# TensorE in emission order through two encoder layers, with the attention steps rearranged and a split final sum

## The chip, the cores and the metric

The kernel runs on one core of a Trainium2 chip. The metric is the device time of the slowest (here the only) core in microseconds, as the median of several runs. The profiled execution is one run of its own, with its own time.

## The reference

Two layers of an encoder work on 16 meta tokens and 256 sequence tokens (T = 272) with 1024 channels, in float32. Each layer takes four token mixers from one normalised input, gates and sums them, and adds a gated feed-forward part:

```
u = rms_norm(h, ln_mix[l])
(aq, ak, av, bq, bk, bv, cq, ck, cv, dq, dzf, dzb, di, dg, gz) = split_in(u @ w_in[l])
y_a = windowed_sink_attention(...)   # 4 heads, relative bias, a sink in the softmax
y_b = axial_rope_attention(...)      # q and k normalised per head, then rotated
y_c = differential_attention(...)    # two softmaxes per head, p0 - lam * p1
y_d = hgrn2_bidirectional(...)       # gated linear recurrence, both directions
gate = sigmoid(gz)                   # 4 x 1024 columns of w_in
merged = sum over n of gate[n] * (y_n @ w_branch[l, n])
h = h + merged @ w_out[l]
u = rms_norm(h, ln_ffn[l])
h = h + (silu(u @ w_ffn_gate[l]) * (u @ w_ffn_up[l])) @ w_ffn_down[l]
out = rms_norm(h, ln_final)[meta tokens dropped]
```

## The kernel before

Every float32 product is made of three matmuls: weights and activations are each split into a high part (rounded to the format that TensorE takes at full pace) and a rest, and high*high, high*rest and rest*high are summed in PSUM. `split_next` (L261 to L279) loads one 512 KB weight tile on the SP queue, casts it on ScalarE (L275) and subtracts on VectorE (L276); `weights` keeps one tile ahead of the one in use, in three buffers. `block` makes one output tile of 128 channels from 24 matmuls of 272 columns (L290 to L292). In the second layer the gate products, branch products and the last feed-forward product are turned round (`prod_t`, L318 to L320), with 512 output columns to a matmul.

A layer begins with 22 projection blocks in the order `ORDER`. Two generators hang on that loop and on the loop after it, and `advance(a, b)` lets each go on by one step when its credit has reached 1:

- `branch_d` is mixer D: a step for the diagonal blocks (`close`, L721 and L733), seven steps for segment lengths 1 to 64 (`close` or `apart`, L749), one for the halves (L801, L802), one for the meta tokens (L815, L824), one for the product with the values (`mix`, L436 and L442) and one for the norm.
- `softmax_stream` is mixers C, B and A, in units of 128 queries. `scores` (L513) makes 12 matmuls on 64 rows each, in two groups of 6, each group into two PSUM tiles. VectorE reduces them, ScalarE takes the exponentials, `normalise` divides, `turn` (L453 to L460) transposes the probabilities, and `mix` multiplies them with the values. `close_unit` ran the division and the turning of a unit one after the other, as two steps, after the next unit's first scores.

`values` (L409 to L427) turns the value rows by transposes (L416) and small products (L425), and `prep_b` (L544 to L577) prepares mixer B's norms (L401, L562, L392). Both were called right after the projection block whose output they read had been scaled on VectorE (L963 or L965).

After the projections comes `MIXING`: gate blocks `g`, and branch products `w` of a mixer that is done. In the second layer `mixing_t` does this, and after each half of the last branch product it transposes the four 128-column tiles of that half of the sum (L889) and splits them (L891, L892) for the output product.

PSUM has two pools of four tiles: `pmm` for the large products and `pat` for everything else.

The order on each engine is made by a planner: it takes the instructions in the order in which the program emits them, but lets a later one go first where, by its own account of times, an earlier one isn't ready. The program on the engine then runs in that order.

The last feed-forward product of the second layer adds, for each of its 22 weight tiles, to four PSUM tiles (2 halves of the tokens by 2 halves of the channels); after it each half of the tokens is added to the rest (L1087), squared (L1089), its norm taken (L1090 to L1092), scaled with the norm and the final weights in one operation (L1094) and sent out (L1095).

Of the kernel before, what the change touches and what calls it, by code (L numbers as in the profile page):

```python
# [15 lines left out]
P = 128  # L16
# [28 lines left out]
RATE_D, RATE_S = 1.0, 1.0  # L45
WAIT_C = (8, 8)
# [35 lines left out]
def trunk(ctx, tc, xT, w_in, w_branch, w_out, w_gate, w_up, w_down, rel_bias, params, consts, masks, onehot, ln_out, out):  # L82
    nc = tc.nc
    V, S, G, PE = nc.vector, nc.scalar, nc.gpsimd, nc.tensor

# [458 lines left out]
    def prep_b(l, pj):  # L544

        src = [pj["bq0"], pj["bq1"], pj["bk"]]
        sqs = []
        for j in range(3):
            t = midt()
            S.activation(out=t, in_=src[j], func=AF.Square)  # L550
            sqs.append(t)
# [92 lines left out]
    def softmax_stream(l, c0, pj, done):  # L644
# [6 lines left out]
        def close_unit(u):  # L651
            n, qt, gen, st = u
            next(gen, None)
            yield
# [23 lines left out]
        for n, qt in units:  # L678
# [6 lines left out]
            next(gen)  # L685
            yield
            if pend:
                yield from close_unit(pend)
            if n == 2:
                next(gen)  # L690
                yield
            pend = (n, qt, gen, st)
        yield from close_unit(pend)


# [155 lines left out]
    def mixing_t(acts, rcol, done, advance):  # L851
# [3 lines left out]
        for kind, b, half in MIXING_T:  # L855
            n = BRANCHES[b]
            if kind == "g":
                pss = [pmm(), pmm()]
                for x in range(4):
# [4 lines left out]
                    advance(RATE_D, RATE_S)  # L864
# [9 lines left out]
            advance(RATE_D, RATE_S)  # L874
# [10 lines left out]
            if b == 3:  # L885
                for m in range(4 * half, 4 * half + 4):
                    ps = pat()
                    for i in range(2):
                        PE.transpose(ps[:, P * i:P * (i + 1)], acc[:, DM * i + P * m:DM * i + P * (m + 1)], ident)  # L889
                    t = slot(F32R)  # L890
                    S.copy(t[:, 0, META:], ps[:, :SEQ])  # L891
                    V.tensor_tensor(out=t[:, 1, META:], in0=ps[:, :SEQ], in1=t[:, 0, META:], op=ALU.subtract)  # L892
                    merged.append(t)
        return merged

    for l in range(DEPTH):
# [32 lines left out]
        for idx, name in enumerate(ORDER):  # L929
            t0 = first_token(l, name)  # L930
            ps = lead[idx] if idx < 3 else block(acts, t0)
            if l == 0 and idx == 3:
                prep_small()
            if name[:2] == "dz":
                d, j = name[2], int(name[3])
                z = midt()
                V.tensor_tensor(out=z[:, t0:], in0=ps[:, t0:T], in1=rstd[:, t0:], op=ALU.mult)
                dd = 0 if d == "f" else 1
                kdst, fdst = dt["KK"][:, 2 * dd + j, :], dt["T1"][:, 2 * (1 - dd) + j, :]
                if t0:  # L940
                    G.memset(kdst[:, :t0], 0.0)
                    G.memset(fdst[:, :t0], 1.0)
                fdst, kdst = fdst[:, t0:], kdst[:, t0:]
                S.activation(out=fdst, in_=z[:, t0:], func=AF.Sigmoid)
                S.activation(out=kdst, in_=z[:, t0:], func=AF.Sigmoid, scale=-1.0)
                if l > 0:
                    c = 2 * dd + j
                    V.tensor_scalar(out=fdst, in0=fdst, scalar1=lbc[:, c:c + 1], scalar2=lb[:, c:c + 1], op0=ALU.mult, op1=ALU.add)
                    V.tensor_scalar(out=kdst, in0=kdst, scalar1=lbc[:, c:c + 1], scalar2=None, op0=ALU.mult)
                V.tensor_scalar(out=fdst, in0=fdst, scalar1=1e-30, scalar2=None, op0=ALU.max)  # L950
                continue
            if name[0] == "d":
                dst = dt[name[1]][:, int(name[2]), :]
            else:
                half = 1 if name[1] == "v" or name[-1] == "1" else 0
                if half == 0:
                    cur = pj[name[:2]] = slot()
                dst = pj[name] = cur[:, half, :]
            scale = {"aq": 0.125, "cq": 32 ** -0.5, "dq": 0.125}.get(name[:2])
            if t0:  # L960
                G.memset(dst[:, :t0], 0.0)
            if scale is None:
                V.tensor_tensor(out=dst[:, t0:], in0=ps[:, t0:T], in1=rstd[:, t0:], op=ALU.mult)  # L963
            else:
                V.scalar_tensor_tensor(out=dst[:, t0:], in0=ps[:, t0:T], scalar=scale, in1=rstd[:, t0:], op0=ALU.mult, op1=ALU.mult)  # L965
            if name == "dg1":
                sg = gslot()
                S.activation(out=sg, in_=dt["g"], func=AF.Sigmoid)
                V.tensor_tensor(out=dt["g"], in0=dt["g"], in1=sg, op=ALU.mult)
            if name == "di1":  # L970
                dt["val", 3] = values([dt["i"][:, 0, :], dt["i"][:, 1, :]])
            if name[1] == "v":
                n = "abc".index(name[0])
                if n == 1:
                    prep_b(l, pj)
                    pj["b"] = parts_of(pj["bq"], pj["bk"])
                elif n == 2:
                    pj["c"] = parts_of(pj["cq"], pj["ck"], True)
                    if l == 0:
                        load_bias("a")  # L980
                pj["val", n] = values([pj[name]])
                pj["ready", n] = True
            advance(RATE_D if idx >= 8 else 0.0, RATE_S if idx >= 10 else 0.0)
        gates, merged = {}, []
        acc = w = None
        for kind, i, m in MIXING if l < DEPTH - 1 else ():
            n = BRANCHES[i]
            if kind == "g":

                if m % 2 == 0:  # L990
                    gates[n, m // 2] = slot()
                g = gates[n, m // 2][:, m % 2, c0:]
                ps = block(acts, c0)
                V.tensor_tensor(out=g, in0=ps[:, c0:T], in1=rstd[:, c0:], op=ALU.mult)
                S.activation(out=g, in_=g, func=AF.Tanh, scale=0.5)
                advance(RATE_D, RATE_S)
                continue
            while n not in done:
                advance(1.0, 1.0)
            if acc is None:  # L1000
                acc = accp.tile([P, KT, T], F32, tag="at", name=nm("acc"))
            if m % 4 == 0:
                w = weights()
                advance(RATE_D, RATE_S)
            ps = pmm()
            for j in range(2):
                prod(ps, w, 2 * (m % 4) + j, done[n][j], c0, j == 0, j == 1)
# [218 lines left out]
```

## Time and profile before

| what | value |
|---|---|
| median of 3 runs | 924.39 us (921.67 to 924.76) |
| the profiled execution | 923.55 us |
| its span, first to last instruction | 921.8 us |
| mean granted TensorE clock | 0.995 |
| TensorE matmul busy | 904.6 us |
| VectorE busy | 666.4 us |
| ScalarE busy | 517.4 us |
| GpSimd busy | 23.1 us |
| DMA | 150.01 MB, mean 163 GB/s |

Busy time of TensorE is that of a pipeline: a matmul counts from its start to its modelled end, and the next one begins before that. So a share near 100% says that there is always one under way, not how densely they follow. The chain of work that ended last is the better view: there each matmul has only the time by which it moved the chain on. The share of the chain by engine, the list of waits and the chain itself are read in that order below.

### The profile page before, as it was taken

To read this page: it belongs to the slowest core of one execution; us is meant where nothing else is said; L and a number is where in the kernel's file an instruction comes from. 1 tells how busy PE (TensorE), PEld (TensorE's weight loads), DVE (VectorE), ACT (ScalarE), POOL (GpSimd) and SP (SyncE) were. 2 spreads that over 40 slices of the span, in tenths; PEclk is the share of its full clock that TensorE was granted. 3 is DMA by queue.
4 is the path that set the end of the run, shared out by engine and by line. 5 is a ranking of instruction groups with operands and counts; after the bars stand their busy time and mean duration, and the time that the engine had idled before them with its cause. 6 is when DMAs were issued, how large, how long until landed. Compare 5 with 4: busy or idle time off the path is not lost.

```text
span 921.8 us, 18150 instructions
## 1 busy us (share of the span) xinstructions
PE 904.6 (98%) x7246; PEld 820.8 (89%) x7246; DVE 666.4 (72%) x1295; ACT 517.4 (56%) x900; POOL 23.1 (3%) x53
## 2 busy tenths in 40 slices
PE   7999999999999999999999999999999999999996
PEld 6989898999999999999999997787788988888885
DVE  6888886858987766665558898767577886677444
ACT  6655766555465444444446568675445676556532
POOL 1520000000000000000000000000000000000000
PEclk9999999999999999999999999999999999999998
DMA  8942344444454555555555423444554655555551
GB/s 309 245 154 76 109 138 138 138 138 153 143 183 162 182 167 179 180 167 180 178 170 177 143 92 115 160 138 159 161 184 156 193 177 183 190 190 191 185 180 46
DMA packets 42613, 150.01 MB, mean 163 GB/s; under 512 B 5024, under 2 KB 5696, under 8 KB 42528
## 3 DMA queue, kind: packets, MB, share of 16 engines
q1 hardware_dynamic: 40896, 144.84, 47.6%
q0 software_dynamic: 1344, 3.48, 1.5%
q8 instruction: 57, 0.93, 0.4%
q10 hardware_dynamic: 288, 0.52, 0.2%
q14 instruction: 28, 0.23, 0.1%
HBM read 147.22 MB, written 1.61 MB: 161 GB/s over the span
## 4 chain that ended last, share of the span: by engine, by line
PE 93%; DVE 4%; ACT 1%; DMA 1%; issue 1%; SPq 0%; DVEq 0%; ACTq 0%
PE pmm L290 18%; PE pmm L292 18%; PE pmm L291 17%; PE pmm L309 8%; PE pmm L318 6%; PE pmm L320 6%; PE pmm L319 6%; PE pmm L310 4%; PE pat L513 2%; PE pat L442 2%; PE pat L453 1%; DVE wlo L276 1%; ACT whi L275 1%; PE pat L721 1%; PE pat L392 1%; DMA h<-in_xT_dram 1%
## 5 line engine op out<-in xcount | busy, mean ns | idle before, releaser
L275 ACT CAST whi<-raw 128x1024 fp32r<-128x1024 f32 (+1 forms) x275 | 284.7, 1039 | 304.6 <-PE pmm L291 125.7
L276 DVE TENSOR_TENSOR wlo<-raw,whi 128x1024 fp32r<-128x1024 f32 (+1 forms) x275 | 332.5, 1212 | 128.4 <-ACT whi L275 125.3
L290 PE MATMUL pmm<-slot,whi 128*128 128x272 f32 (+1 forms) x1232 | 359.9, 293 | 6.3 <-ACT slot L335 5.6
L292 PE MATMUL pmm<-slot,wlo 128*128 128x272 f32 (+1 forms) x1232 | 356.1, 290 | 0.8 <-DVE wlo L276 0.8
L291 PE MATMUL pmm<-slot,whi 128*128 128x272 f32 (+1 forms) x1232 | 356.3, 290 | 0.1
L290 PEld LDWEIGHTS pmm<-slot,whi 128*128 128x128 f32 x1232 | 233.2, 189 | 12.9 <-ACT slot L335 6.0
L291 PEld LDWEIGHTS pmm<-slot,whi 128*128 128x128 f32 x1232 | 234.1, 190 | 2.2 <-DVE slot L336 1.3
L292 PEld LDWEIGHTS pmm<-slot,wlo 128*128 128x128 f32 x1232 | 233.4, 190 | 2.7 <-DVE wlo L276 1.2
L309 PE MATMUL pmm<-slot,whi 128*128 128x512 f32 x320 | 111.9, 394 | 0.2 <-DVE mid L1051 0.2
L310 PE MATMUL pmm<-slot,wlo 128*128 128x256 f32 x320 | 89.5, 280 | 0.0
L318 PE MATMUL pmm<-whi,slot 128*128 128x512 f32 x184 | 73.3, 398 | 0.0
L320 PE MATMUL pmm<-wlo,slot 128*128 128x512 f32 x184 | 73.0, 397 | 0.0
L309 PEld LDWEIGHTS pmm<-slot,whi 128*128 128x128 f32 x320 | 60.1, 188 | 14.0 <-ACT whi L275 0.4
L319 PE MATMUL pmm<-whi,slot 128*128 128x512 f32 x184 | 72.2, 392 | 0.0
L310 PEld LDWEIGHTS pmm<-slot,wlo 128*128 128x128 f32 x320 | 60.3, 188 | 0.0
L318 PEld LDWEIGHTS pmm<-whi,slot 128*128 128x128 f32 x184 | 34.6, 188 | 9.2 <-issue 1.3
L320 PEld LDWEIGHTS pmm<-wlo,slot 128*128 128x128 f32 x184 | 34.5, 188 | 7.7 <-issue 0.3
L319 PEld LDWEIGHTS pmm<-whi,slot 128*128 128x128 f32 x184 | 34.6, 188 | 7.6
L1051 DVE TENSOR_TENSOR mid<-pmm,rstd 128x272 f32<-128x272 f32 (+1 forms) x48 | 20.8, 439 | 24.9 <-PE pmm L292 24.8
L290 PE MATMUL pmm<-y,whi 128*128 128x272 f32 x128 | 37.2, 291 | 0.0
L292 PE MATMUL pmm<-y,wlo 128*128 128x272 f32 x128 | 36.9, 288 | 0.0
L291 PE MATMUL pmm<-y,whi 128*128 128x272 f32 x128 | 36.8, 288 | 0.0
(267 smaller groups left out, 1037.0 us busy)
## 6 DMA issues: line engine op xcount, KB each, us to landing
raw<-in_w_in_dram SPq DMA_DIRECT2D x106, 512.0 KB, 3.5
raw<-in_w_gate_dram SPq DMA_DIRECT2D x44, 512.0 KB, 3.8
raw<-in_w_up_dram SPq DMA_DIRECT2D x44, 512.0 KB, 3.6
raw<-in_w_down_dram SPq DMA_DIRECT2D x44, 512.0 KB, 3.6
raw<-in_w_branch_dram SPq DMA_DIRECT2D x16, 512.0 KB, 3.5
raw<-in_w_out_dram SPq DMA_DIRECT2D x16, 512.0 KB, 3.9
biasA<-scr POOLq DMA_DIRECT2D x8, 136.0 KB, 5.5
h<-in_xT_dram SPq DMA_DIRECT2D x3, 272.0 KB, 5.2
```

What stands on the lines that cost most here:

```text
L275: S.copy(hi[:, sl], raw[:, sl])
L276: V.tensor_tensor(out=lo[:, sl], in0=raw[:, sl], in1=hi[:, sl], op=ALU.subtract)
L290: PE.matmul(o, hi[:, sl], act[:, 0, c0:], start=first, stop=False)
L291: PE.matmul(o, hi[:, sl], act[:, 1, c0:], start=False, stop=False)
L292: PE.matmul(o, lo[:, sl], act[:, 0, c0:], start=False, stop=last)
L309: PE.matmul(ps[:, :2 * SEQ], hi[:, sl], acts[k][:, :, META:], start=k == 0, stop=False, skip_group_check=True)
L310: PE.matmul(ps[:, :SEQ], lo[:, sl], acts[k][:, 0, META:], start=False, stop=k == n - 1, skip_group_check=True)
L318: PE.matmul(o, a, hi[:, sl], start=first, stop=False)
L319: PE.matmul(o, b, hi[:, sl], start=False, stop=False)
L320: PE.matmul(o, a, lo[:, sl], start=False, stop=last)
L442: PE.matmul(ps[64 * hh:64 * hh + 64, c0:T], vn[:, i, vc:vc + 64], pT[i][:, hd, c0:], start=False, stop=i == 1, skip_group_check=True)
L1051: V.tensor_tensor(out=t[:, c0:], in0=ps[:, c0:T], in1=rstd[:, c0:], op=ALU.mult)
```

## The change

In words:

- From the first projection to the last branch product of each layer, TensorE's instructions run in the order in which the program emits them (`manual_schedule` for that engine alone). The other engines keep their planner.
- `values` and `prep_b` are no longer called right after their projection but put on a list, `later`; one entry is taken after the following block (`catch_up`). The squares of `prep_b` (`squares_b`) stay where they were.
- In `softmax_stream` the scores and the division of a unit are one step (for mixer C two, for its two score sets); `turned`, the turning and what follows it, comes after the next unit's scores. The stream has 25 steps in the first layer instead of 37, and 18 instead of 27 in the second.
- The stream waits 11 steps at its beginning instead of 8. It advances by 1 per projection block, and then by 0.85 per block in the first layer and 0.6 in the second; before it was 1 throughout.
- In the mixing the step after a `w` block comes behind its products instead of ahead of them.
- The transposes of the sum in the second layer come behind both halves of the last branch product, and those of the second half outside the ordered region.
- The last product takes 20 weight tiles as before and the last two quarter by quarter, so that each quarter's sum is complete 6 matmuls before the next. The final weights are multiplied ahead of the norm, on GpSimd for the first half of the tokens and on VectorE for the second; the norm is applied by ScalarE on one half of the channels and VectorE on the other; the two output queues are exchanged.

```diff
-RATE_D, RATE_S = 1.0, 1.0
-WAIT_C = (8, 8)
+RATE_D, RATE_S = 1.0, (0.85, 0.6)
+WAIT_C = (11, 11)
...
-        def close_unit(u):
-            n, qt, gen, st = u
-            next(gen, None)
-            yield
+        def turned(u):
+            n, qt, st = u
...
-            next(gen)
+            for k in range(2 if n == 2 else 1):
+                next(gen)
+                if n == 2 and k == 0:
+                    yield
+            next(gen, None)
             yield
             if pend:
-                yield from close_unit(pend)
-            if n == 2:
-                next(gen)
-                yield
-            pend = (n, qt, gen, st)
-        yield from close_unit(pend)
+                yield from turned(pend)
+            pend = (n, qt, st)
+        yield from turned(pend)
...
+        def take(n, tiles):
+            def f():
+                (dt if n == 3 else pj)["val", n] = values(tiles)
+            later.append(f)
+        def take_b():
+            prep_b(l, pj, pj["b_sq"])
+            pj["b"] = parts_of(pj["bq"], pj["bk"])
+            pj["ready", 1] = True
+        def catch_up():
+            if later:
+                later.pop(0)()
+        with tc.manual_schedule(engines={PE_ENGINE}):
+            for idx, name in enumerate(ORDER):
+                ps = lead[idx] if idx < 3 else block(acts, t0)
+                catch_up()
...
+                advance(RATE_D if idx >= 8 else 0.0, 1.0 if idx >= 10 else 0.0)
...
+            if l == DEPTH - 1:
+                merged, merge = mixing_t(acts, rcol, done, advance, catch_up)
         if l == DEPTH - 1:
-            merged = mixing_t(acts, rcol, done, advance)
+            merge(1)
...
-    for k in range(NFF):
+    quarters = [(i, half) for i in range(2) for half in range(2)]
+    for k in range(NFF - 2):
         w = weights()
...
+    ws = [weights(), weights()]
     for i in range(2):
...
         for half in range(2):
+            for x, k in enumerate((NFF - 2, NFF - 1)):
+                prod_t(pss[i][half], ws[x], HALF * half, ff[k], i, False, x == 1)
             V.tensor_tensor(out=o[half], in0=o[half], in1=pss[i][half][:, :HALF], op=ALU.add)
             S.activation(out=sq, in_=o[half], func=AF.Square, accum_out=ss[:, half:half + 1])
+            (G if i == 0 else V).tensor_tensor(out=o[half], in0=o[half], in1=g, op=ALU.mult)
...
-            V.scalar_tensor_tensor(out=o[half], in0=o[half], scalar=r, in1=gB[...], op0=ALU.mult, op1=ALU.mult)
-            (nc.scalar if half else nc.sync).dma_start(...)
+        S.activation(out=o[0], in_=o[0], func=AF.Copy, scale=r)
+        V.tensor_scalar(out=o[1], in0=o[1], scalar1=r, scalar2=None, op0=ALU.mult)
+            (nc.sync if half else nc.scalar).dma_start(...)
```

## Rows read from the trace of the kernel before

**Rows 1.** The page: busy time and share; and the chain's shares by engine.

```profile
PE 904.6 (98%) x7246; PEld 820.8 (89%) x7246; DVE 666.4 (72%) x1295; ACT 517.4 (56%) x900; POOL 23.1 (3%) x53
...
PE 93%; DVE 4%; ACT 1%; DMA 1%; issue 1%; SPq 0%; DVEq 0%; ACTq 0%
```

**Rows 2.** Waits: who waited for whom, us in total, times, longest.

```profile
PE pmm L290 <- ACT slot L335: 5.6, 2, 4.4
...
PEld pat L416 <- DVE slot L963: 1.9, 2, 1.3
```

**Rows 3.** The chain from 96 to 100 us: start, time, what.

```profile
96.67 0.57 PE pat L513 x6
97.25 0.32 PE pmm L290
97.57 0.12 PE pmm L291
...
97.94 0.57 PE pat L513 x3
```

**Rows 4.** The chain: score runs whole and in pieces, elsewhere.

```profile
91.75 0.56 PE pat L513 x4
...
117.94 0.58 PE pat L513 x6
...
180.89 0.95 PE pat L513 x12
...
557.29 0.58 PE pat L513 x6
...
579.63 1.33 PE pat L513 x9
581.39 0.56 PE pat L513 x3
```

**Rows 5.** Busy time by stretch: the first layer's attention and what follows it; us, then PE, PEld, DVE, ACT.

```profile
92.00:235.00 143.00, 142.83 (x1161) 128.34 (x1159) 109.03 (x285) 87.80 (x187) 0.15 (x2) 1.00 0.42 136
235.00:250.00 15.00, 15.00 (x121) 15.00 (x121) 14.23 (x28) 7.18 (x10) 0.00 (x0) 1.00 0.35 118
```

**Rows 6.** Instructions in order of time, 80 to 90 us, by engine (ACT, PE, DVE).

```profile
80.98 1.28 ACT L404 ACT_TABLE_LOAD   x1
...
85.21 0.38 PE L802 MATMUL pat<-p,p 64*128 64x128 f32 x2
89.23 0.62 PE L815 MATMUL pat<-p,p 64*32 64x256 f32 x4
...
89.11 0.28 DVE L810 TENSOR_SCALAR p<-p,tot 128x128 f32<-128x128 f32 x1
```

**Rows 7.** Instructions in order of time around 702 us.

```profile
702.20 0.40 PE L290 MATMUL pmm<-slot,whi 128*128 128x256 f32 x2
702.26 1.41 DVE L892 TENSOR_TENSOR slot<-pat,slot 128x256 fp32r<-128x256 f32 x4
```

**Rows 8.** The end: last matmul and last DMA issue.

```profile
913.07 0.40 PE L320 MATMUL pmm<-wlo,y 128*128 128x512 f32 x1
...
918.67 0.34 ACTq L1095 DMA_DIRECT2D out_dram<-hT  x1
```

**Rows 9.** Groups by line: busy us, mean ns.

```profile
L1087 DVE TENSOR_TENSOR hT<-hT,pmm 128x512 f32<-128x512 f32 x4 | 2.7, 688 | 4.1 <-PE pmm L320 4.1
L1094 DVE SCALAR_TENSOR_TENSOR hT<-hT,col,p 128x512 f32<-128x512 f32 x4 | 2.8, 748 | 0.1
L1089 ACT ACTIVATE p<-hT 128x512 f32<-128x512 f32 x4 | 2.5, 626 | 6.1 <-DVE hT L1087 6.1
L1089 ACT ACTIVATION_READ_ACCUMULATOR p<-hT 128x1 f32 x4 | 0.7, 186 | 0.0
L1091 ACT ACTIVATE col<-col,cst 128x1 f32<-128x1 f32 x2 | 0.6, 294 | 1.5 <-DVE col L1090 1.5
L241 POOL TENSOR_SCALAR_AFFINE_SELECT biasA<-biasA 128x1024 f32<-128x1024 f32 x1 | 1.9, 1945 | 1.1 <-DMA biasA<-scr 1.1
```

More of the change, by code (lines that the diff above doesn't have):

```diff
@@ L84, in trunk @@
     V, S, G, PE = nc.vector, nc.scalar, nc.gpsimd, nc.tensor
+    PE_ENGINE = mybir.EngineType.PE
     one = ctx.enter_context(tc.tile_pool(name="one", bufs=1))
@@ L542, in parts_a, with squares_b, prep_b @@
         st["p"] = p
-    def prep_b(l, pj):
-        src = [pj["bq0"], pj["bq1"], pj["bk"]]
[L547 to L551, printed above, removed]
+    def squares_b(pj):
+        sqs = []
+        for n in ("bq0", "bq1", "bk"):
+            t = midt()
+            S.activation(out=t, in_=pj[n], func=AF.Square)
+            sqs.append(t)
+        return sqs
+    def prep_b(l, pj, sqs):
+        src = [pj["bq0"], pj["bq1"], pj["bk"]]
         rh = head_cols(sqs[:2])
@@ L849, in trunk, with mixing_t @@
     gl = ctx.enter_context(tc.tile_pool(name="gl", bufs=1))
-    def mixing_t(acts, rcol, done, advance):
+    def mixing_t(acts, rcol, done, advance, catch_up):
         gates, merged = {}, []
@@ L884, in mixing_t, with merge @@
                     V.tensor_tensor(out=a, in0=a, in1=g, op=ALU.add)
[L885 to L894, printed above, removed]
+            advance(RATE_D, RATE_S[1])
+        def merge(half):
+            for m in range(4 * half, 4 * half + 4):
+                ps = pat()
+                for i in range(2):
+                    PE.transpose(ps[:, P * i:P * (i + 1)], acc[:, DM * i + P * m:DM * i + P * (m + 1)], ident)
+                t = slot(F32R)
+                S.copy(t[:, 0, META:], ps[:, :SEQ])
+                V.tensor_tensor(out=t[:, 1, META:], in0=ps[:, :SEQ], in1=t[:, 0, META:], op=ALU.subtract)
+                merged.append(t)
+        merge(0)
+        return merged, merge
     for l in range(DEPTH):
@@ L927, in advance @@
                     next(gen, None)
[L929 to L939, printed above, removed]
-                if t0:
[L941 to L991, printed above, removed]
-                g = gates[n, m // 2][:, m % 2, c0:]
[L993 to L1007, printed above, removed]
-            g = gates[n, m // 2][:, m % 2, c0:]
-            if i == 0:
-                V.scalar_tensor_tensor(out=acc[:, m, c0:], in0=g, scalar=1.0, in1=ps[:, c0:T], op0=ALU.add, op1=ALU.mult)
-            else:
-                t = midt()
-                V.scalar_tensor_tensor(out=t[:, c0:], in0=g, scalar=1.0, in1=ps[:, c0:T], op0=ALU.add, op1=ALU.mult)
-                V.tensor_tensor(out=acc[:, m, c0:], in0=acc[:, m, c0:], in1=t[:, c0:], op=ALU.add)
-            if i == 3:
-                merged.append(split_from(acc[:, m, :], c0, slot))
@@ L1077, in trunk @@
     pss = [[pmm() for _ in range(2)] for _ in range(2)]
-    for k in range(NFF):
+    quarters = [(i, half) for i in range(2) for half in range(2)]
+    for k in range(NFF - 2):
         w = weights()
-        for i in range(2):
-            for half in range(2):
-                prod_t(pss[i][half], w, HALF * half, ff[k], i, k == 0, k == NFF - 1)
+        for i, half in quarters:
+            prod_t(pss[i][half], w, HALF * half, ff[k], i, k == 0, False)
+    ws = [weights(), weights()]
     for i in range(2):
@@ L1089, in trunk @@
             S.activation(out=sq, in_=o[half], func=AF.Square, accum_out=ss[:, half:half + 1])
+            g = gB[:, HALF * half:HALF * (half + 1)]
+            (G if i == 0 else V).tensor_tensor(out=o[half], in0=o[half], in1=g, op=ALU.mult)
         V.tensor_tensor(out=r, in0=ss[:, 0:1], in1=ss[:, 1:2], op=ALU.add)
@@ L1092, in trunk @@
         V.reciprocal(out=r, in_=r)
+        S.activation(out=o[0], in_=o[0], func=AF.Copy, scale=r)
+        V.tensor_scalar(out=o[1], in0=o[1], scalar1=r, scalar2=None, op0=ALU.mult)
         for half in range(2):
-            V.scalar_tensor_tensor(out=o[half], in0=o[half], scalar=r, in1=gB[:, HALF * half:HALF * (half + 1)], op0=ALU.mult, op1=ALU.mult)
-            (nc.scalar if half else nc.sync).dma_start(out=out[P * i:P * (i + 1), HALF * half:HALF * (half + 1)], in_=o[half])
+            (nc.sync if half else nc.scalar).dma_start(out=out[P * i:P * (i + 1), HALF * half:HALF * (half + 1)], in_=o[half])
 def _constants():
```

91 lines of the change are left out of this document (88 added, 3 removed).

## The prediction

> **What bounds the kernel now.** I read the page first. TensorE is busy 98% of the span, VectorE 72%, ScalarE 56% [rows 1]. Since busy time of TensorE is a pipeline's, the second view is the chain that ended last: 93% of it is TensorE, 4% VectorE [rows 1]. The third is the list of waits: TensorE's matmuls waited 5.6 us for a first activation, most of it at the start, and its weight loads 1.9 us, in two places, for the scaling in front of `values` (L416 on L963) [rows 2]; no other wait of TensorE's reaches 1.4 us in total. So between the first blocks and the last matmul there is no waiting to win but those 1.9 us. What is left is how closely matmuls follow one another, and that is read in the chain itself [rows 3]: within a block each 272-column matmul moves the chain on by 0.12 us, so 24 of them take 3.0 us, but the first one behind a group on 64 rows takes 0.32. A run of 6 score matmuls takes 0.57, and 12 in one go take 0.95 [rows 4]. So 6 more cost 0.38, entering costs 0.57 - 0.38 = 0.19, and leaving 0.32 - 0.12 = 0.20. A run of 3 takes the same 0.57 as one of 6 [rows 3]: the two halves of the rows work side by side only where both have a matmul. The last thing to read is the end: the last matmul begins at 913.07 and is over by 913.5, while the last output is issued at 918.67 [rows 8].
>
> **Scores in one piece.** Today the planner cuts score runs and puts block matmuls between. The first layer's 48 score matmuls of mixer C are nine runs in the chain, from the one at 91.75 to the one at 117.94 [rows 4], of 5.4 us in sum; four runs of 0.95 are 3.8. That is 1.6. Of the five extra exits three fall to neighbours that are small products too, or transposes; two at least go, 0.4. In the second layer one set of scores runs as 0.58 + 0.57 + 0.57 (the first at 557.29) and one as 1.33 + 0.56 (579.63 and 581.39) [rows 4], against 0.95 each: 0.8 and 0.9, and two exits of 0.2. Together 1.6 + 0.4 + 0.8 + 0.9 + 0.4 = 4.1. In emission order each `scores` call is one run of 12, if the four PSUM tiles of `pat` are free. I take 4.0; bounds are 0 (if it waits for those tiles as long as the other work in the cuts took) and 4.8 (the two L815 runs in one piece and `values` not mixed into `close` as well).
>
> **`values` and `prep_b` one block later.** The two waits of 1.9 us [rows 2] go, since a block of 3.0 us on TensorE now covers the scaling on VectorE. Nothing is late for it: the first reader of a value tile is `mix`, at least three blocks on.
>
> **Turning two steps later, steps spread by a rate.** `normalise` and its ScalarE work get a block or two more ahead of the transposes. The first layer's stream has 25 working steps at 0.85 per block, 24 / 0.85 + 1 = 29 blocks instead of 37, so the same VectorE work lies in less time. Bound: from 109.03 us in 143 [rows 5] take away eight blocks' weight split and scaling, 8 x (1.21 + 0.44, means of L276 and of the scaling in the groups by line) = 13, and 8 x 3.0 of time: 96 in 119, or 81%, beside 76% now. From 235 to 250 VectorE has 14.23 of 15 while TensorE loses nothing [rows 5]. So I cost density at 0. In the second layer 18 steps at 0.6 take 30 blocks, more than the 27 now: 0 too.
>
> **TensorE in emission order.** Nothing can be put into a gap any more. Where did the planner use that? At the meta step of mixer D: L815 begins at 89.23, when the preceding step's last matmuls began at 85.21 [rows 6], with a rest of a block and 18 matmuls of the next (18 x 0.125 = 2.2 us) drawn ahead of it, because the scalings L808 and L810 came late on VectorE, the last at 89.11 [rows 6], behind `prep_b`. After the change `prep_b` and this step are issued together, behind the same block. `prep_b` also takes three PSUM tiles, which come free behind a 1.28 us table load on ScalarE [rows 6], and L815 and L824 want three more of the four. Cost: between 0 (its VectorE work needs nothing of TensorE and may run earlier) and 2.2 per layer; I take 1.3 in the first and 0.7 in the second, which has no L824. Queued behind the waiting matmul is everything of TensorE's, and VectorE and ScalarE soon after. For steps that want more than four `pat` tiles at once (`values` and scores in the first mixing block, `values` and `close`) I add 0.7, between 0 and one 0.57 run each, five of them: 2.9. Together 2.7, from 0 to 7.3.
>
> **Sum of the second layer's mixers.** The first eight transposes (L889) no longer lie among the last branch matmuls. Today the first output matmul starts at 702.20 and the first rest is subtracted from 702.26 on [rows 7], that is, just in time. With the transposes behind the matmuls, the cast (0.39) and one subtraction (0.35) are no longer covered. Cost 0.6; from 0 to 1.5 (if the second half waits as well).
>
> **The end.** The last quarter's sum is complete with the last matmul, as now. After it: adding 0.69, squaring 0.63 and reading 0.19, adding two columns 0.15, root 0.29, reciprocal 0.16, scaling by at most 0.75 [rows 9] (the small ones are means of the same stretch), in all 2.9 if VectorE is free, and issue at E + 2.9. In between VectorE has the two multiplications by the final weights (0.72 each by L1094), each behind its square, since it writes over what that reads. One of them can come ahead of the last addition and one ahead of the column sum, so E + 2.9 to E + 4.6. Now it is 918.67 - 913.5 = E + 5.2. Gain 0.6 to 2.3; I take 1.2. The GpSimd multiplication of 512 columns is not in the trace; the nearest is a one-input pass over 1024 in 1.95 [rows 9], so 1.0 to 2.0. It begins at about E - 1.4 and is over by E + 0.6, beside the second half's work; only if VectorE's scaling of the first half stands ahead of the last addition does it cost up to 0.5.
>
> The Trainium skill (GPSIMD Engine Reference, section 4.1 Engine selection) puts two-input elementwise work at about twice VectorE's time. By that the multiplication would take some 1.5 us (estimate, from 0.75), and the sum would be the same. No run so far shows it.
>
> **Sum**, against the profiled execution of 923.55 (span 921.8 and 1.75 around it): -4.0 - 1.9 + 2.7 + 0.6 - 1.2 = -3.8, or 919.75. The profiled execution is 0.84 below the median 924.39, inside the spread of the three; I forecast **919.8**.
>
> **Rivals.**
> 1. *No new waits.* All of 2.7 + 0.6 stays away: 923.55 - 7.1 = 916.5. For it: VectorE's share is below that of stretches without loss [rows 5]. Against: the order of L815 [rows 6].
> 2. *The order costs what it saves.* Waits at their upper bound, 7.3: 923.55 - 4.0 - 1.9 - 1.2 + 0.6 + 7.3 = 924.4, no change. For it: the planner did cut these runs for some reason. Against: the C steps no longer lie beside mixer D, where five of the nine cuts were.
> 3. *Slower: TensorE waits at score steps for PSUM.* The place is the second group of 6 in `scores`; it needs the two tiles that VectorE has to empty from the step before. If each of the 16 whole runs of both layers waits for two reductions (0.43 + 0.08 each in the groups by line, 1.0 us), 16 more are paid: 923.55 - 3.8 + 16 = 935.8; at half of it, 927.8. It decides from 3.8 / 16 = 0.24 us per run on. Against: five of the runs now already go through in one piece of 0.95, as that at 180.89 [rows 4].
> 4. *Only the end and `values` count*, the ordered region changes nothing: 923.55 - 3.1 = 920.5, inside the forecast's range.
>
> The Trainium skill (TensorE: Matmul & The Clock Gate, Part 2, Step-by-step) says that matmuls stay in program order and only weight loads are drawn ahead. That is what makes rival 3 dear: one waiting matmul holds all behind it. This trace agrees as far as it goes: at L416 both the weight load and all blocks behind it stood still [rows 2].
>
> **How the numbers follow.** Forecast with rival 4, 0.59; rival 1, 0.12; rival 2, 0.17; rival 3, 0.12. No measurement of this kernel tells less than about 0.3% from no change, which is 2.8 us: faster means below 921.6, slower above 927.2. Of the forecast's 0.59 I give 0.52 to below 921.6; with rival 1 that makes 0.64 for faster. Within: 0.07 and most of rival 2, 0.23. Slower: 0.13, which is rival 3 and the end of rival 2. The range reaches from rival 1 less 1 us, 915.5, to rival 2 plus 1, 925.5.
>
> **What would show it.** L416 has no wait left; score runs are 12 long, 0.95 each, none of 3; the chain between matmul ends and last DMA issue is about 4 us. It is wrong if L513 or L815 appear among TensorE's waits with more than 3 us in sum, if TensorE's share of the chain falls below 92%, or if the last matmul ends later than it does now.

## The result, and the profile after

The changed kernel takes **918.86 us** (median of 7 runs, 917.29 to 920.86) against 923.76 for the kernel before (7 runs, 921.67 to 924.76): ratio 0.9949, 95% interval 0.9934 to 0.9963. The forecast was 919.8. The profiled execution took 920.86, which is the longest of the seven; so its rows show somewhat more loss than the median run has.

The page, with what answers to [rows 1] (all line numbers after are those of the changed kernel: L290 has become L291, L416 is L417, L513 is L514, L815 is L817, L824 is L826, L892 is L896):

```profile
PE 900.9 (98%) x7246; PEld 820.2 (89%) x7246; DVE 665.9 (72%) x1295; ACT 514.2 (56%) x898; POOL 25.8 (3%) x55
...
PEclk9998999999999999999999999999999999999999
...
PE 93%; DVE 4%; ACT 2%; issue 1%; DMA 1%; SPq 0%; ACTq 0%; DVEq 0%
```

The shares say nothing new: TensorE still has 93% of the chain. One digit does: in the fourth slice, 69 to 92 us, the granted clock is below 0.9. The list of TensorE's waits (who waited for whom, us in total, times, longest) answers to [rows 2]:

```profile
PE pmm L291 <- ACT slot L336: 6.0, 2, 4.6
PE pat L723 <- ACT whi L276: 1.0, 1, 1.0
PE pmm L293 <- DVE wlo L277: 0.9, 1, 0.9
PE pat L514 <- DVE col L613: 0.8, 2, 0.4
PE pat L893 <- DVE slot L896: 0.7, 1, 0.7
PE pat L826 <- ACT hr L405: 0.7, 1, 0.7
PE pmm L291 <- ACT slot L895: 0.3, 1, 0.3
```

The wait in front of `values` (L417) is gone. New are L723 (mixer D's diagonal blocks, 1.0 us), L514, L826, and the pair L893 and L291 at the merge (each below 1 us). L723 stands in the place of the longer of the two old waits: before, L416 waited there, now L723 does (start, time, engine, line; in brackets idle time and what ended it; the first row is of the kernel before):

```profile
55.48 0.44 PE L416 MATMUL pat<-cst,slot 128*128 128x128 f32 x2 [1.11 <-DVE slot L963]
...
53.58 0.73 PE L723 MATMUL pat<-p,gk 64*32 64x32 f32 x63 [1.02 <-ACT whi L276]
```

As far as waits go, `values` one block later thus removed one of its two waits and exchanged the other.

The chain of the changed kernel from 100 to 124 us answers to [rows 4] (start, time, what):

```profile
104.53 0.95 PE pat L514 x10
...
112.36 0.62 PE pat L514 x6
...
113.48 0.64 PE pat L514 x5
...
117.32 0.96 PE pat L514 x12
...
121.48 1.06 PE pat L514 x12
```

These are four runs of 12 where nine pieces stood before (the first counts 10 on the chain; the trace has all 12). The second, in two parts, is the place where `values` and the scores of one step together want more PSUM tiles than the four of `pat`. All 16 runs of both layers are whole, two of them with such a gap (0.70 us from one matmul's start to the next, of which 0.4 is wait).

Where [rows 6] showed mixer D's meta step late, the instructions in order of time now show this (start, time, engine, line; in brackets idle time and what ended it):

```profile
82.27 0.27 DVE L812 TENSOR_SCALAR p<-p,tot 128x128 f32<-128x128 f32 x1
...
84.53 1.28 ACT L405 ACT_TABLE_LOAD   x1
...
84.82 0.64 PE L817 MATMUL pat<-p,p 64*32 64x256 f32 x8
...
85.83 0.27 ACT L405 ACTIVATE hr<-pat,cst 128x8 f32<-128x8 f32 x1
...
86.15 2.36 PE L826 MATMUL pat<-p,p 64*128 64x16 f32 x16 [0.69 <-ACT hr L405]
```

The last scaling on VectorE (L812) is over at 82.54, long before L817; before, it began at 89.11. So L817 waits for nothing. L826 does: ScalarE loads a table (1.28) ahead of the root that empties the PSUM tile of `prep_b`. Then comes what the forecast did not have. Busy time by stretch (us, PE, PEld, DVE, ACT, POOL, granted clock, DMA share, GB/s):

```profile
84.00:86.00 2.00, 1.46 (x22) 0.53 (x21) 2.00 (x6) 1.97 (x4) 0.00 (x0) 1.00 0.46 127
86.00:88.00 2.00, 1.85 (x15) 1.85 (x15) 2.00 (x14) 0.87 (x5) 0.00 (x0) 0.66 0.35 135
88.00:90.00 2.00, 2.00 (x10) 1.96 (x10) 1.75 (x4) 0.42 (x1) 0.00 (x0) 0.50 0.00 0
90.00:92.00 2.00, 2.00 (x10) 2.00 (x10) 0.26 (x1) 0.00 (x0) 0.00 (x0) 0.50 0.52 137
92.00:94.00 2.00, 2.00 (x12) 1.93 (x11) 0.00 (x0) 0.14 (x1) 0.00 (x0) 0.63 0.31 125
```

Behind a row of small products and the wait the granted clock falls to its lower level, 1.2 GHz (0.50), and is back at 2.4 GHz only within the last of these rows. A block's matmuls then run 10 to 2 us instead of 16. From 88 us on the busy column reads 2.00 of 2.00: busy time cannot show this, the clock column does. How long the clock is low differs from run to run: the mean granted clocks of the seven runs reach from 0.994 to 0.998, with a median of 0.996; the profiled one has 0.995.

At the merge (where [rows 7] were "just in time"):

```profile
699.57 0.61 PE L291 MATMUL pmm<-slot,whi 128*128 128x256 f32 x3 [0.30 <-ACT slot L895]
...
700.41 0.42 DVE L896 TENSOR_TENSOR slot<-pat,slot 128x256 fp32r<-128x256 f32 x1
...
700.89 0.33 PE L893 MATMUL pat<-cst,acc 128*128 128x128 f32 x1 [0.70 <-DVE slot L896]
```

The first output matmul and the ninth transpose wait 1.0 us together. The end answers to [rows 8] and [rows 9]:

```profile
909.17 2.67 POOL L1125 TENSOR_TENSOR hT<-hT,p 128x512 f32<-128x512 f32 x2 [306.63 <-ACT p L1123]
...
911.35 0.40 PE L321 MATMUL pmm<-wlo,y 128*128 128x512 f32 x1
...
913.45 0.68 DVE L1125 TENSOR_TENSOR hT<-hT,p 128x512 f32<-128x512 f32 x1
...
914.05 0.15 DVE L1126 TENSOR_TENSOR col<-col 128x1 f32<-128x1 f32 x1
...
915.57 0.34 ACTq L1132 DMA_DIRECT2D out_dram<-hT  x1
```

From the last matmul's end, about 911.75, to the last issue it is 3.8 us, where it was 5.2.

### The profile page after: what moved, and what is told of

It is laid out like the page before. It is cut to its first block, busy times and chain, and to the rows that moved or that the text cites. A ratio compares the mean times of both kernels' runs of the same rounds, so it can differ in the third digit from the quotient of the medians.

```text
span 919.1 us, 18144 instructions
## 1 busy us (share of the span) xinstructions
PE 900.9 (98%) x7246; PEld 820.2 (89%) x7246; DVE 665.9 (72%) x1295; ACT 514.2 (56%) x898; POOL 25.8 (3%) x55
## 4 chain that ended last, share of the span: by engine, by line
PE 93%; DVE 4%; ACT 2%; issue 1%; DMA 1%; SPq 0%; ACTq 0%; DVEq 0%
PE pmm L291 18%; PE pmm L293 18%; PE pmm L292 18%; PE pmm L310 8%; PE pmm L319 6%; PE pmm L321 6%; PE pmm L320 6%; PE pmm L311 4%; PE pat L514 2%; PE pat L443 2%; PE pat L454 1%; PE pat L723 1%; DVE wlo L277 1%; DMA raw<-in_w_in_dram 1%; PE pat L437 1%
## 5 line engine op out<-in xcount | busy, mean ns | idle before, releaser
L277 DVE TENSOR_TENSOR wlo<-raw,whi 128x1024 fp32r<-128x1024 f32 (+1 forms) x275 | 332.8, 1213 | 123.1 <-ACT whi L276 121.7
L291 PE MATMUL pmm<-slot,whi 128*128 128x272 f32 (+1 forms) x1232 | 361.1, 294 | 6.3 <-ACT slot L336 6.0
L293 PE MATMUL pmm<-slot,wlo 128*128 128x272 f32 (+1 forms) x1232 | 356.1, 289 | 0.9 <-DVE wlo L277 0.9
L291 PEld LDWEIGHTS pmm<-slot,whi 128*128 128x128 f32 x1232 | 234.0, 190 | 14.6 <-ACT slot L336 6.4
L293 PEld LDWEIGHTS pmm<-slot,wlo 128*128 128x128 f32 x1232 | 234.3, 190 | 1.7 <-DVE wlo L277 1.1
L291 PE MATMUL pmm<-y,whi 128*128 128x272 f32 x128 | 37.1, 290 | 0.0
L293 PE MATMUL pmm<-y,wlo 128*128 128x272 f32 x128 | 36.9, 288 | 0.0
```

The costliest lines, as they stand in the source:

```text
L277: V.tensor_tensor(out=lo[:, sl], in0=raw[:, sl], in1=hi[:, sl], op=ALU.subtract)
L291: PE.matmul(o, hi[:, sl], act[:, 0, c0:], start=first, stop=False)
L293: PE.matmul(o, lo[:, sl], act[:, 0, c0:], start=False, stop=last)
```

## The experiments

Each was timed 4 to 11 times, beside the kernel before on the same chip. The chips differ by some tenths, so the ratios are compared, not the medians.

**1. The end alone**, in the kernel before.

```diff
-    for k in range(NFF):
+    for k in range(NFF - 2):
...
+            (G if i == 0 else V).tensor_tensor(out=o[half], in0=o[half], in1=g, op=ALU.mult)
```

> The kernel before with the new end alone (last two weight tiles quarter by quarter, final weights multiplied ahead of the norm, queues exchanged). If the end is worth what the two profiles show (last matmul to last DMA issue 5.2 us before, 3.8 after): 1.4 us faster, about 922.4 against 923.8, ratio 0.9985. If the last quarters are bought with a later last matmul, or the end of the span is set by the landing of the outputs: 0. Everything up to the last matmul should lie as before.

Measured: 922.76 (before 923.92), ratio 0.9987 [0.9978, 0.9996]. The end is worth 1.2 us.

**2. The planner's order** with everything else of the change.

```diff
-        with tc.manual_schedule(engines={PE_ENGINE}):
+        if True:
```

> The changed kernel without the ordered region: TensorE's order is the planner's again, all else as changed. If the emission order itself pays, through score runs in one piece: pieces of L514 come back and it is 2 to 4 us slower than the changed kernel, 921 to 923. If the rearranged steps pay and the order doesn't matter: as the changed kernel, 918.9. If the order costs more in waits than it saves (the waits at L826, L514, L723 and the stretch at half clock behind L826): faster than the changed kernel, 915 to 917.

Measured: 916.57 (before 923.92), ratio 0.9925 [0.9912, 0.9938]. Without its emission order the change is faster by 2.2 us (0.0024 x 923.55), the third of the three cases; the two intervals just overlap. In the order that the planner writes, 14 of 16 score runs are whole by themselves. And at the meta step it keeps half a block between the small products:

```profile
84.44 0.64 PE L817 MATMUL pat<-p,p 64*32 64x256 f32 x8
85.00 0.40 PE L291 MATMUL pmm<-slot,whi 128*128 128x272 f32 x1
...
86.71 1.53 PE L826 MATMUL pat<-p,p 64*128 64x16 f32 x16
```

L826 has no wait, takes 1.53 instead of 2.36, and in this profile the clock stays whole. Its runs have a median clock of 0.998; one has 0.995, and that one took 918.81, so the planner's order isn't always spared. The start of the n-th matmul into a `pmm` tile, changed kernel less this one, is 0.4 us at n = 360, 4.0 at n = 480 and 4.2 at n = 5400: in these two profiles nearly the whole difference arises around this one step.

**3. The emission order alone**, in the kernel before.

```diff
+        with tc.manual_schedule(engines={mybir.EngineType.PE}):
             for idx, name in enumerate(ORDER):
```

> The kernel before with the ordered region around projections, mixing and branch products and nothing else changed. If the steps had to be rearranged for the order to be bearable: TensorE waits at L416 for the scaling (1.9 us as before or more), at L453 for the division of the unit before (up to 1 us at each of 15 units) and at L459, 5 to 15 us slower than before, 929 to 939. If emission order alone is the gain: 919 to 921.

Measured: 941.98, ratio 1.0198 [1.0182, 1.0214], slower by 18 us, above the 929 to 939 that were expected. Two rows of its waits:

```profile
PE pat L416 <- DVE slot L964: 6.3, 8, 2.2
...
PEld pat L453 <- ACT p L480: 2.2, 2, 2.0
```

With the old steps, where a step's matmuls read what was issued just before, the order holds TensorE up eight times in `values` and at the turnings; in sum TensorE's waits are some 14 us longer than in the kernel before. What was not foreseen is the clock: its four runs have mean clocks of 0.987 to 0.990, where the kernel before beside it has 0.995 to 0.998. So the 18 us are not the price of waits alone.

**4. The meta step ahead of `prep_b`**, in the changed kernel.

```diff
-                catch_up()
+                if idx != 18:
+                    catch_up()
...
+                if idx == 18:
+                    catch_up()
```

> The changed kernel, but behind the nineteenth projection block the step of mixer D (L817, L826) is issued ahead of mixer B's preparation (L402, L566, L393), not behind it. If the wait at L826 for a PSUM tile (0.7 to 1.2 us in the changed kernel's profile) and the stretch at half clock that followed it (86.6 to 93.5 us, some 2.5 us lost) come from that order: both gone, 2 to 3.5 us faster than the changed kernel, about 916. If the stretch at half clock comes from something else and is in some runs only: 0.5 to 1 us faster, 918.

Measured: 918.15, ratio 0.9946 [0.9933, 0.9959], no different from the change, so the first theory's 916 missed. The wait at L826 is gone, but the small products still stand in one row, and the clock still falls:

```profile
86.00:88.00 2.00, 2.00 (x12) 1.80 (x9) 1.68 (x11) 1.00 (x3) 0.00 (x0) 0.57 0.00 0
88.00:90.00 2.00, 2.00 (x12) 2.00 (x11) 1.02 (x3) 0.00 (x0) 0.00 (x0) 0.57 0.00 0
```

So the wait is not needed for the fall. `PE pmm L293 <- DVE wlo L277` rose to 1.9 us besides.

**5. A block between `prep_b` and the meta step**, emission order kept.

```diff
-                advance(RATE_D if idx >= 8 else 0.0,
+                advance(RATE_D if idx >= 8 and (l, idx) != (0, 18) else 0.0,
```

> The changed kernel, emission order kept, with the meta step of mixer D in the first layer (and with it the rest of mixer D) put off by one block, so that take_b's small products and those of the meta step are no longer neighbours. Theory 'one place': the emission-order region loses its 2.3 us against the planner's order (918.86 against 916.57) only behind this step, by the 0.7 us wait at L826 and the half-clock stretch behind it; then no wait at L826, the clock whole between 84 and 95 us, and about 916.5 (ratio 0.992). Rival 'everywhere': the region costs a little at many steps, and the time stays at 918 to 919 (0.994 to 0.995). Rival 'late D': the block products that need mixer D start late and the time is above 919.

Measured: 919.43 (before 923.21), ratio 0.9960 [0.9947, 0.9974]. All three theories missed. In the profile the clock is whole from 80 to 131 us and L826 doesn't wait, as 'one place' said; but the rest of mixer D comes one block later, and its norm now meets the scores of mixer C in one block:

```profile
PE pat L514 <- ACT mid L361: 1.7, 1, 1.7
...
PE pat L514 <- DVE col L613: 1.1, 2, 0.7
```

Here two steps that want the four `pat` tiles at once cost waits of 0.4 to 1.7 us where they meet. This is the mechanism of the third rival, at single places.

**6. The old start and rates**, planner's order.

```diff
-RATE_D, RATE_S = 1.0, (0.85, 0.6)
-WAIT_C = (11, 11)
+RATE_D, RATE_S = 1.0, (1.0, 1.0)
+WAIT_C = (8, 8)
```

> The changed kernel under the planner's order (no emission-order region), with the old start and rate of the attention stream (wait 8, rate 1.0 in both layers). In the order that the planner writes, scores are then cut again: 28 pieces against 18 with the new start and rates, 24 in the kernel before. Theory 'density': the planner cuts score runs where the steps come too close, so the new start and rates are what put scores in one piece; ten pieces more at 0.19 for entering, 0.20 for leaving where a block follows, and the score products that run on one half of the rows alone: 3 to 4.5 us, 919.6 to 921. Rival 'turning': the gain comes from turning later and from values, and the rate is worth nothing: 916 to 917.5.

Measured: 924.48, ratio 1.0014 [1.0005, 1.0023]. The later start and the lower rate are worth 8 us in this place (0.0089 x 923.55), twice what the theory gave. No wait of TensorE's over 0.9 us is new; in the profile its score runs are in 29 pieces, where experiment 2 has 18, with the same attention steps. So the later start and the lower rate are what keeps the scores whole. More on this below.

**7. `values` and `prep_b` at once**, planner's order.

```diff
-            later.append(f)
+            f()
...
-                        later.append(take_b)
+                        take_b()
```

> The changed kernel under the planner's order, with values and the preparation of mixer B issued at once behind their projection, as before, and not one block later. Theory 'the waits of values': TensorE waits again about 1.9 us in front of values (weight load, for the scaling on VectorE), and the time is 918 to 919. Rival 'no worth': the planner draws other work ahead of them (all score runs are 12 long in its order here), nothing waits, 916 to 917.

Measured: 919.09, ratio 0.9963 [0.9950, 0.9975], close to the theory's 918 to 919: slower by 3.5 us, of which one row is

```profile
PE pat L417 <- DVE slot L988: 2.2, 2, 1.9
```

The L723 wait, 1.2 us in experiment 2, is not there, so waits explain 1.0 us of the 3.5. All 16 score runs are whole in this profile, so cut scores are not the rest; it stays open.

**8. The old attention steps** with the new start and rates, planner's order: `softmax_stream` as in the kernel before.

```diff
-        def turned(u):
-            n, qt, st = u
+        def close_unit(u):
+            n, qt, gen, st = u
+            next(gen, None)
+            yield
```

> The changed kernel under the planner's order, with the attention stream's steps as before: normalisation in the step after the scores, turning one step after that, no yield before a mixer's last step. Its score runs are cut exactly as with the new steps (18 pieces). Theory 'no worth of its own': the number of pieces decides, and the time is 916 to 917.2. Rival 'turning': transposes wait for the scaling of probabilities (ScalarE and VectorE) by 0.2 to 0.3 us in each of 14 turnings, and the time is 919 to 921.

Measured: 927.82, ratio 1.0053 [1.0041, 1.0066]: 11.8 us slower, with the same 18 pieces of scores. Both theories missed. In the profile the matmuls behind the first layer's attention start 8.7 us later than experiment 2's. The first row is at that place, at 236.9 us; the second is the same thing at the end of the second layer's stream, at 697 us:

```profile
PE pat L454 <- ACT p L481: 3.3, 1, 3.3
...
PE pat L437 <- DVE pTm L461: 2.1, 1, 2.1
```

The clock falls at the first place as well:

```profile
235.00:240.00 5.00, 2.87 (x19) 2.28 (x19) 3.04 (x13) 2.53 (x7) 0.00 (x0) 0.58 0.62 205
240.00:245.00 5.00, 4.59 (x20) 2.25 (x20) 0.71 (x4) 0.39 (x1) 0.00 (x0) 0.50 0.00 0
```

The old stream has 37 steps in the first layer, and from a start 3 steps later at 0.85 per block it isn't through when the blocks run out. The last steps then follow each other with nothing between (`while n not in done`), and each waits for the one before. So this run does not measure the turning. It shows two things: the old steps keep the scores as whole as the new ones at this start and rate, and fewer steps are what lets the stream finish in time at that rate.

**9. Emission order everywhere but in the first layer's projections**

```diff
-        with tc.manual_schedule(engines={PE_ENGINE}):
+        with tc.manual_schedule(engines={PE_ENGINE}) if l else nullcontext():
             for idx, name in enumerate(ORDER):
...
+        with tc.manual_schedule(engines={PE_ENGINE}):
             gates, merged = {}, []
```

> The changed kernel with TensorE in emission order everywhere but in the projections of the first layer, which are left to the planner; so the step of mixer D behind take_b is in the planner's hands again, and the rest is in emission order. Theory 'one place': the whole difference between the changed kernel and the planner's order arises between the 360th and the 480th block matmul (in the profiles 3.6 of 4.2 us), so the time is that of the planner's order, ratio 0.992 to 0.993, about 916.5. Rival 'everywhere': the ordered mixing blocks and the second layer cost too, and the time stays at 0.994 to 0.995, 918 to 919.

Measured: 916.40 (before 923.01), ratio 0.9927 [0.9914, 0.9940]: the planner's 0.9925 again. The theory 'one place' holds as far as these runs can tell: the order costs in the first layer's projections and nowhere else. That it is the meta step among these 22 blocks is read from the two profiles of experiment 2.

**10. All old steps, start and rate**; new are the later `values`, the merge, the place of the step behind a `w` block, and the end. Beside the diff of experiment 8:

```diff
-RATE_D, RATE_S = 1.0, (0.85, 0.6)
-WAIT_C = (11, 11)
+RATE_D, RATE_S = 1.0, (1.0, 1.0)
+WAIT_C = (8, 8)
```

> The changed kernel under the planner's order with the attention stream wholly as before: old steps, old turning, wait 8 and rate 1.0; new are only values and the preparation of mixer B one block later, and the end. Scores are cut into 26 pieces here (18 with the new steps). Theory 'the three belong together': fewer steps are what allow the late start and the low rate, and these keep the scores whole; together they are worth the 3.7 to 4.3 us that pieces and prices gave, so the time is 916.6 + 4 = 920.3 to 921, ratio 0.9965. Rival 'turning and rate each count': the new steps bring their singly measured 11 and 8 us in part, and the time is above 922. Rival 'the rest is values': 918 to 919.

Measured: 922.06, ratio 0.9990 [0.9981, 0.9999]; just inside the range of the rival 'turning and rate each count' (above 922); the theory 'the three belong together' (0.9965) missed. This is the end alone (0.9987) and nothing more, so the rearranged steps are worth 0.9990 - 0.9925, 6.0 us, as a whole. The L416 waits are gone here too, and mixer D's diagonal blocks wait 1.2 us in their place, as in experiment 2. The chain shows what the planner does with the old steps:

```profile
88.27 0.58 PE pat L514 x6
...
89.80 0.57 PE pat L514 x3
...
90.68 0.57 PE pat L514 x3
```

One score set in three pieces of 0.57, 1.7 us for what takes 0.95 when whole; the next set, from 95.50 on, goes the same way.

**11. and 12. What the rows suggested**: planner's order; the transposes of each half of the merge behind that half again; and two other ends. In the first the last quarter's product goes to a tile of its own; in the second GpSimd takes three of the four products, the last quarter takes norm and weights in one operation, and the first tokens' scaling leaves ScalarE.

```diff
-        merge(0)
-        return merged, merge
+            if b == 3:
+                merge(half)
+        return merged
```

The end of the eleventh, and of the twelfth:

```diff
+            t = o[half]
+            if i == 1 and half == 1:
+                o[half] = slot().rearrange("p a b -> p (a b)")[:, :HALF]
+            (G if i == 0 else V).tensor_tensor(out=o[half], in0=t, in1=g, op=ALU.mult)
```

```diff
-            (G if i == 0 else V).tensor_tensor(out=o[half], in0=o[half], in1=g, op=ALU.mult)
+            if i == 0 or half == 0:
+                G.tensor_tensor(out=o[half], in0=o[half], in1=g, op=ALU.mult)
```

> The changed kernel under the planner's order, with two more edits: the eight transposes of each half of the second layer's merge stand behind that half again, as before, and in the last quarter the product by the final weights goes to a tile of its own, so that it need not wait for the square and lies beside it. Theory: the merge loses 0.75 us less (1.55 against 0.8 between 695 and 710 us), the end gains the 0.67 of a multiplication: 916.6 - 1.4 = 915.2, ratio 0.991. Rival: VectorE has other work at either place, and only half of it is seen: 915.9. Rival: the earlier transposes are cut into the blocks and cost as much: 916.0 to 916.6.

> The changed kernel under the planner's order with the merge put back as in e11_best, and another end: no multiplication by the final weights stands on VectorE or ScalarE behind the last addition any more. GpSimd takes that of the first tokens and of the second tokens' first half, the last quarter takes norm and weights in one operation behind the norm, and the first tokens' scaling and both its outputs leave ScalarE. Theory: from the last matmul's end to the last DMA issue it is 2.9 us instead of 3.8 (addition 0.69, square 0.63 and 0.19, two columns 0.15, root 0.29, reciprocal 0.17, scaling 0.72), so 914.5 (ratio 0.9905). Rival 'VectorE is still in the way' (the first tokens' two scalings, 0.96 behind the last addition): 3.2 us, 914.9. Rival 'GpSimd is late' (three passes of 1.33 from about 905.6 on, the third over at 909.5 or later): 3.8 as before, 915.5.

Measured: 915.47 (before 923.01), ratio 0.9915 [0.9900, 0.9929]; and 915.68 (before 923.42), 0.9917 [0.9903, 0.9930]. Both beat the kernel before and the change; against the planner's order (0.9925) they are ahead by 0.7 to 0.9 us, which the intervals don't separate. In the profiles the merge gains 0.7, as foreseen: eleven's block matmuls lag experiment 2's by 1.32 us before it and by 0.60 behind it. Eleven's end gains nothing (last matmul over at 908.13, last issue at 911.96, 3.8 again), because the product keeps its place ahead of the column sum on VectorE. Twelve's gains 0.3 (last matmul over at 906.01), between its two rivals:

```profile
906.65 0.16 DVE L1129 RECIPROCAL col<-col 128x1 f32<-128x1 f32 x1
...
906.91 1.22 DVE L1132 TENSOR_SCALAR hT<-hT,col 128x512 f32<-128x512 f32 x2
...
908.05 0.15 DVE L1127 TENSOR_TENSOR col<-col 128x1 f32<-128x1 f32 x1
...
909.57 0.37 ACTq L1137 DMA_DIRECT2D out_dram<-hT  x1
```

The first tokens' scalings (L1132) start behind the reciprocal of their own norm (L1129); by then GpSimd's products of the first tokens are done. They stand ahead of the column sum (L1127). That is its rival 'VectorE is still in the way'.

## Why the prediction was right, and where not

The time came out 0.9 us below the forecast, but its terms were off by up to 2.0, and the errors in part cancelled, so the closeness of the number is partly luck. Effects below are differences of ratios times 923.55, so they add up to the whole by construction; each is uncertain by 1 to 2 us.

| term | forecast | measured | from |
|---|---|---|---|
| scores and steps | -4.0 | -6.0 | experiments 2 and 10 |
| `values` and merge together | -1.9 + 0.6 | +0.3 | 10 and 1 |
| emission order | +2.7 | +2.2 | result and 2 |
| end | -1.2 | -1.2 | 1 |
| sum | -3.8 | -4.7 | result |

**Scores in one piece.** The mechanism was right: the runs are whole, 12 in 0.95 us. But it was put down to the emission order, and that is the step which failed: under the planner the same steps keep 14 of 16 runs whole (experiment 2), and the order without the new steps makes the kernel 18 us longer (3). What keeps the scores whole is the stream's later start and lower rate: with them there are 18 pieces with the old steps too (8), without them 29 with the new steps (6). The shorter stream is what makes them affordable. Why the size was too small was not tried by itself. The forecast priced score runs alone; other small groups were cut less often too. Counted over the whole profile, TensorE changes between a matmul into `pmm` and one into `pat` 194 times in experiment 10, 170 in 2 and 164 in the changed kernel. At the 0.19 and 0.20 of [rows 3] and [rows 4] for entering and leaving, 24 fewer are an estimated 4.7 us of the 6.0. In the same way experiment 6, with 200, should lose 1.2 us to experiment 10, and loses 2.2. But the count doesn't hold everywhere: experiment 1 has 180 and runs no faster than 10 with its 194, and 7 has the 170 of experiment 2 and is 3.5 us slower. So the count can be one part of the price; the rest stays open.

**`values` later.** The two waits at `values` went, as foreseen, in every kernel with this edit, but one of them came back in front of mixer D's diagonal blocks (L723, 1.0 us here, 1.2 in experiments 2 and 10; every profile with this edit has it, with 0.3 to 1.2 us, and none without). The forecast lacked that. With the old steps the edit was worth nothing that the runs tell from zero: experiments 1 and 10 are 0.9987 and 0.9990, the merge's loss included. In their profiles 10 is 1.8 us ahead behind the first layer, but most of that is a stretch at 1.2 GHz that experiment 1's profile has behind its longest L416 wait (clock 0.50 from 56 to 58 us); 0.7 is lost at the merge. With the new steps it is worth 3.5 us (7). A term's price held only beside the other edits.

**Density** was put at nothing, by a bound of 81% for VectorE. The stretch of [rows 5] now shows 75%, and no wait of TensorE's on it but those above:

```profile
92.00:235.00 143.00, 142.58 (x1178) 129.41 (x1178) 107.68 (x282) 86.10 (x186) 0.15 (x2) 0.99 0.40 128
```

**Emission order.** The sum was near, the place wrong. Forecast were waits behind late VectorE work at L815, 1.3 and 0.7, and 0.7 for `pat` tiles. L817 waits nowhere, since mixer D's scalings are now over in time; L826 waits 0.7 for the tile behind the table load, which the forecast named as a side matter; the rest goes with the lower clock behind it, which it lacked. In the profiles the second layer loses nothing. The clock's part is argued from profiles and mean clocks (median 0.996 here, 0.998 in experiments 2 and 9), and no run changes the clock alone. Its fall at this place is seen without the wait (4) and not seen in the profiles where a block or half a block parts the small products (2, 5, 9).

**Merge.** Forecast 0.6; in the profiles it is 0.7 (11), by the cast and subtraction named. **End.** Forecast 1.2, measured 1.2; 3.8 us from matmul to issue where "about 4" stood. Of the signs that were to show the forecast wrong none came: L514 and L817 have 0.8 us of waits, below 3; the chain's share is 93%; the last matmul is over 1.7 us earlier.

**Rivals.** The first (no new waits, 916.5) meets the time of the planner's order, 916.57, but by other terms. The second didn't come: the order costs 2.2 us, not 7.3. The third, PSUM waits at score steps, did not decide (two gaps of 0.70; seven runs, not five, already took 0.94 or 0.95 before), but it is what undid experiment 5. The fourth (only the end and `values` count) did not hold: experiment 10, which has both, gains 0.9 us and not 3.1. The Trainium skill (TensorE: Matmul & The Clock Gate, Part 2, Step-by-step) says that matmuls stay in program order. Experiment 3's trace agrees: where the steps aren't arranged for that, eight waits at L416 alone hold TensorE for 6.3 us.

## What to carry to other kernels

Before an order is forced, run the same rearranged steps under the planner: here the steps made 6.0 us of the gain and the end 1.2, and the forced order gave 2.2 back, as far as the profiles show at one place. A later start and a lower rate kept small matmuls in whole runs here, and fewer steps let the stream finish in time at that rate. When a wait is gone, look whether the next instruction now waits in its place. When many small products meet in one row, look at the granted clock behind them, since waits and busy shares can show nothing there (experiment 4).

## What the runs showed of the hardware

- The granted clock fell to 1.2 GHz behind a row of small products (L402, L566, L393, L817, L826 within 83 to 88.5 us) also where TensorE had no wait (experiment 4: 0.57 from 86 to 90 us), and in the profiles it did not with half a block or a block between them (1.00 in 2, 5 and 9). In 2 us at that level 10 block matmuls ran instead of 16. How long it is low differs from run to run of one kernel: the seven runs of the changed kernel have mean clocks of 0.994 to 0.998.
- GpSimd's product of two 128x512 operands took 1.30 us where VectorE's took 0.68:

```profile
L1125 POOL TENSOR_TENSOR hT<-hT,p 128x512 f32<-128x512 f32 x2 | 2.6, 1302 | 306.7 <-ACT p L1123 306.6
L1125 DVE TENSOR_TENSOR hT<-hT,p 128x512 f32<-128x512 f32 x2 | 1.4, 678 | 0.0
```

  The Trainium skill (GPSIMD Engine Reference, section 4.1 Engine selection) puts such work at about twice VectorE's time; the trace agrees, 1.9.
